# Cutting the fourth tile, placing the final norm by estimates, and storing the output in half-megabyte pieces

## The chip, the cores and the metric

The kernel runs on all eight cores of one Trainium2 chip, one launch, with the same program on each core. The metric is the device time of the slowest core in microseconds (us). Most runs of one kernel agree within 0.3%. A second, slower state appears in some runs whatever the kernel is: the cores of one die show a lower granted TensorE clock and the run is some per cent longer.

Engines are named as in the profile: PE is the TensorE matmul, PEld its weight load, DVE is VectorE, ACT is ScalarE, POOL is GpSimd, SP is SyncE. SPq and ACTq are the queues on which SyncE and ScalarE issue transfers. A *tile* below is one of five groups of token columns, of 256, 512, 512, 512 and 272 columns; a *chunk* is one of eight groups of 128 channels. "The fourth tile" has index 3.

## The reference, cut to what matters

Two decoder layers; each core takes one prompt of 2048 tokens and 16 of the sample tokens. Only the very end is touched by the change: the last feed-forward down projection, its residual add, and the final RMS norm over the 1024 channels.

```python
def rmsnorm(x, g):
    xf = x.astype(jnp.float32)
    y = xf * lax.rsqrt(jnp.mean(xf * xf, axis=-1, keepdims=True) + EPS)
    return (y * g.astype(jnp.float32)).astype(x.dtype)
# ... (mixers, first layer) ...
        x = x + mix
        h = rmsnorm(x, norm_ffn[layer])
        x = x + swiglu(h, ffn_w_gate[layer], ffn_w_up[layer], ffn_w_down[layer])
    return rmsnorm(x, norm_final), ...
```

## The kernel before

Channels lie on partitions and tokens along the free dimension, so the mean over channels needs a sum over partitions. ACT squares each chunk, POOL adds the squares of most chunks into one accumulator, and matmuls with a matrix of ones add what is left and spread the sum to all partitions. ACT then takes Ln and Exp(-0.5 x) to get the reciprocal root ("rstd") in a PSUM bank, and for the chunks that POOL multiplies a second Exp puts it into an SBUF buffer `gtmp` (POOL's chunks get the gain earlier, in a copy on ACT). DVE multiplies the other chunks by gain and rstd at once.

All of this is dripped into the loop of the projection, so that the norm of tile n runs while PE projects tile n+1. In the traces below each engine runs its work in the order in which the program emits it: on core 4, for one, ACT has the Ln and two Exp of `mid`, then the square of chunk 4, its gain copy and the squares of chunks 5, 6 and 7 at 1322.04, 1322.78, 1323.47, 1323.96, 1324.48, 1324.90 and 1325.22 us, and then the gain copy of chunk 7 at 1326.05.

```python
class Norm:
    def square(self, n, c): ...      # ACT Square; POOL adds chunks 0..5; chunks 6, 7 ("direct") go to PE
    def mid(self, n):                # ones-matmuls, Ln, Exp -> gtmp, Exp -> bank; queue 8 multiplies
        ...
    def on_pool(self, n, c):
        return self.final and c in ((1, 4, 7) if n == 4 else (7,))

    POPS = (2, 1, 1, 0, 1, 1, 1, 1)
    POPS4 = (1, 1, 1, 1, 0, 0, 1, 1)

    def step(self, n, m):            # after each chunk m of the projection of tile n
        self.square(n, m)
        if self.on_pool(n, m):       # gain copy on ACT
            sc.op("act", ...Copy, scale=gain...)
        self.pop((self.POPS4 if n == 4 else self.POPS)[m])   # DVE multiplies of the tile before
        if n < 4 and m == 7:
            self.pop_pool(1)

    def before(self, n, m):
        if m == 4 and n > 0:
            self.mid(n - 1)

    def last(self):
        self.mid(4)
        self.pop_pool()
        self.pop(KC)

    def store(self, n, c):
        done = self.stored.setdefault(n, set())
        done.add(c)
        if n < 4:
            if len(done) == KC:      # the whole tile in one store: up to 2 MB
                out_evs.append(sc.dma("sp", o_y[:, xrange_(n)], xT[:, xrange_(n)], ...))
        elif c ^ 1 in done:          # the last tile: four stores of two chunks, 272 KB
            lo = c & ~1
            q_, s_ = ("sp", "out") if lo % 4 == 0 else ("act", "out2")
            ...

def ffn_dn2(l, ga, gb, nm):          # the last down projection
    use_banks(6)
    for n in range(5):
        for m in range(KC):
            nm.before(n, m)
            ...                      # matmuls of chunk m, six per column group
            xacc(bk, bkB, m, n)      # DVE: residual add
            nm.step(n, m)
    nm.end()
    pending[4] = nm.last
```

Of the kernel before, what the change touches and what calls it, by code (L numbers as in the profile page):

```python
# [7 lines left out]
BF16 = mybir.dt.bfloat16  # L8
ALU = mybir.AluOpType
AF = mybir.ActivationFunctionType  # L10
# [5 lines left out]
D = 1024  # L16
KC = 8
SEQ = 2048
NS = 16
T = SEQ + NS  # L20
TT = [(0, 256), (256, 512), (768, 512), (1280, 512), (1792, 272)]
LASTP = (1792, 256)
XOFF = [KC * sum(w_ for _, w_ in TT[:n_]) for n_ in range(len(TT))]
DFF = 2816
# [256 lines left out]
def build_program():  # L281
# [32 lines left out]
    with contextlib.ExitStack() as st:  # L314
        sc = Sched(nc, st, self_sync=SELF_SYNC)

        def sb(name, shape, dt):
            return st.enter_context(nc.sbuf_tensor(name, list(shape), dt))
# [73 lines left out]
        def merge(dsts, srcs):  # L392
            for s_ in srcs:
                evs = ([s_.w] if s_.w is not None else []) + list(s_.r.items())
                for d_ in dsts:
                    for (k_, v_) in evs:
                        if d_.r.get(k_, 0) < v_:
                            d_.r[k_] = v_
# [3 lines left out]
        acc = [sqf[:, i * 512:(i + 1) * 512] for i in range(2)]  # L402
        accb = [sqall[:, i * 1024:i * 1024 + 512] for i in range(2)]
        rng = [sqall[:, 2048 + i * 512:2048 + (i + 1) * 512] for i in range(2)]
        drc = [sqall[:, 3072 + i * 512:3072 + (i + 1) * 512] for i in range(2)]
        accB = [Buf(f"acc{i}") for i in range(2)]
        rngB = [Buf(f"rng{i}") for i in range(2)]
# [5 lines left out]
        def nxt(kind, n):  # L413
            i = st_[kind]
            st_[kind] = (i + 1) % n
            return i
# [153 lines left out]
        def drip(k_):  # L570
            if active:
                active[0].pop(k_)
                if not active[0].q:
                    active.pop()
                    use_banks(8)

        class Norm:

            def __init__(self, gcol, final=False, direct=()):
                self.gcol = gcol  # L580
                self.final = final
                self.direct = direct
                self.q = []
                self.parts = {}
                self.stored = {}
# [53 lines left out]
            def emit(self, n, c):  # L639
                c0, w = TT[n]  # L640
                out = xs(c, n) if self.final else hT[:, c, c0:c0 + w]
                pl = self.on_pool(n, c)
                r_, rB_ = (gtmp[n % 2], gtmpB[n % 2]) if pl else (banks[6 + n % 2], bankB[6 + n % 2])
                if pl:
                    sc.op("pool", lambda E: E.tensor_tensor(
                        out=out, in0=xs(c, n), in1=r_[:, 0:w], op=ALU.mult),
                        reads=[xB[c][n], rB_], writes=[xB[c][n]])
                else:
                    sc.op("dve", lambda E: E.scalar_tensor_tensor(  # L649
                        out=out, in0=xs(c, n), scalar=vecs[:, self.gcol + c:self.gcol + c + 1],  # L650
                        in1=r_[:, 0:w], op0=ALU.mult, op1=ALU.mult),
                        reads=[xB[c][n], rB_, cB["vecs"]],
                        writes=[xB[c][n] if self.final else hB[c][n]])
                if self.final:
                    self.store(n, c)
# [14 lines left out]
            POPS = (2, 1, 1, 0, 1, 1, 1, 1)  # L670
            POPS4 = (1, 1, 1, 1, 0, 0, 1, 1)

            def step(self, n, m):
                self.square(n, m)
                if self.on_pool(n, m):
                    sc.op("act", lambda E: E.activation(
                        out=xs(m, n), in_=xs(m, n), func=AF.Copy,
                        scale=vecs[:, self.gcol + m:self.gcol + m + 1]),
                        reads=[xB[m][n], cB["vecs"]], writes=[xB[m][n]])
                self.pop((self.POPS4 if n == 4 else self.POPS)[m])  # L680
                if n < 4 and m == 7:
                    self.pop_pool(1)

            def before(self, n, m):
                if m == 4 and n > 0:
                    self.mid(n - 1)

# [3 lines left out]
                    self.pop(KC)  # L691

            def last(self):
                self.mid(4)
                if self.final:
                    self.pop_pool()
                    self.pop(KC)
                else:
                    active.append(self)
# [14 lines left out]
        def proj(bk, bkB, wt, wtB, wcol, n, src=None, srcB=None, nk=KC, wstride=None):  # L714
            c0, w = TT[n]
            if src is None:
                need_h(n)
            src_ = hT if src is None else src
            srcB_ = hB if srcB is None else srcB

            def f(E):
                last = None
                for k in range(nk):
                    o = k * wstride + wcol
                    last = E.matmul(bk[:, 0:w], lhsT=wt[:, o:o + 128], rhs=src_[:, k, c0:c0 + w],  # L725
                                    start=(k == 0), stop=(k == nk - 1))
                return last
            wtBs = list(wtB) if isinstance(wtB, (list, tuple)) else [wtB]
            sc.op("pe", f, reads=wtBs + [srcB_[k][n] for k in range(nk)], writes=[bkB])

        def xacc(bk, bkB, m, n):
            c0, w = TT[n]
            sc.op("dve", lambda E: E.tensor_tensor(  # L733
                out=xs(m, n), in0=bk[:, 0:w], in1=xs(m, n), op=ALU.add),
                reads=[bkB, xB[m][n]], writes=[xB[m][n]])

        def out_proj(prefix, nm, slots=None):
            if slots is None:
                slots = [w_acquire(f"{prefix}_{h}") for h in range(2)]
            use_banks(6)  # L740
            for n in range(5):
                for m in range(8):
                    wt, wtB = slots[m // 4]
                    nm.before(n, m)
                    bk, bkB = nbank()
                    proj(bk, bkB, wt, wtB, (m % 4) * 128, n, src=mix, srcB=mB, wstride=512)
                    xacc(bk, bkB, m, n)
                    nm.step(n, m)
            nm.end()
            pending[4] = nm.last  # L750
            w_release()
            w_release()
# [49 lines left out]
        def ffn_dn2(l, ga, gb, nm):  # L802
            wa, waB = w_acquire(f"dn{l}_{ga}")
            wb, wbB = w_acquire(f"dn{l}_{gb}")
            parts = [(wa, 4 * (ga % 2), len(groups[ga])), (wb, 4 * (gb % 2), len(groups[gb]))]
            tot = sum(p_[2] for p_ in parts)
            use_banks(6)
            for n in range(5):
                c0, w = TT[n]
                for m in range(KC):  # L810
                    nm.before(n, m)
                    bk, bkB = nbank()

                    def f(E, bk=bk, m=m, c0=c0, w=w):
                        last = None
                        i = 0
                        for (wt_, s0, nch_) in parts:
                            for jl in range(nch_):
                                last = E.matmul(bk[:, 0:w],  # L819
                                                lhsT=wt_[:, jl * 1024 + m * 128: jl * 1024 + (m + 1) * 128],  # L820
                                                rhs=mix[:, s0 + jl, c0:c0 + w], start=(i == 0), stop=(i == tot - 1))
                                i += 1
                        return last
                    sc.op("pe", f, reads=[waB, wbB] + [mB[s0 + jl][n] for (_, s0, nch_) in parts for jl in range(nch_)],
                          writes=[bkB])
                    xacc(bk, bkB, m, n)
                    nm.step(n, m)
            nm.end()
            pending[4] = nm.last
            w_release()  # L830
            w_release()
# [3 lines left out]
        def ffn(l, nm):  # L835
            G = len(groups)
            ffn_up(l, 0)
            for g in range(1, G):
                ffn_up(l, g)
                if g == G - 1:  # L840
                    act_warm_lnexp()
                    break
                ffn_dn(l, g - 1)
                if l == 0 and g - 1 == 2:
                    w_issue_special("v_1")
            ffn_dn2(l, G - 2, G - 1, nm)

        act_warm_lnexp()
        nbk = {}
# [240 lines left out]
        merge(gtmpB, SB[1:3])  # L1090

        merge(accB + bsB_, sqB)
        out_proj("out0", Norm(VC_NFFN + 0, direct=(7,)), out0)
        merge([wsTB], [SB[3]])
        late_setup()
        ffn(0, Norm(VC_NMIX + 8, direct=(6, 7)))

        wv0, wv0B = w_acquire("v_0")
        wv1, wv1B = w_acquire("v_1")
# [110 lines left out]
                w_release()  # L1210

        act_warm_lnexp()
        out_proj("out1", Norm(VC_NFFN + 8, direct=(7,)))

        out_evs = [ev_pp, ev_ps, ev_cp, ev_cs, ev_v]
        ffn(1, Norm(VC_NFIN, final=True, direct=(6, 7)))
        flush_pending()
        sc.wait("sp", [("out", sc.cnt["out"]), ("out2", sc.cnt["out2"])])
        sc.emit_all()
# [80 lines left out]
```

## Time and profile before

| | before |
|---|---|
| time, median of four runs | 1341.91 us |
| span of the profiled core (4) | 1340.1 us |
| spans of the eight cores | 1338.6 to 1340.1 us |
| granted TensorE clock | 0.991 to 0.993 |
| last projection matmul to end of span | 18.5 us |

The first and the fourth part of the page of the kernel before: busy time of each engine with its share of the span and its instructions, and the chain of waits by engine.

```profile
PE 1289.1 (96%) x7283; PEld 717.6 (54%) x7386; DVE 673.5 (50%) x1190; ACT 346.7 (26%) x669; POOL 168.5 (13%) x213
...
PE 88%; DVE 5%; issue 2%; DMA 1%; ACT 1%; POOL 1%; DVEq 0%; SPq 0%; ACTq 0%; POOLq 0%
```

PE is the limit of the kernel as a whole, but the change leaves all PE work before the last projection as it is. What matters is the stretch in which PE has nothing left to do. The timeline of the kernel before on core 4 shows it; the columns are start in us, busy time, engine, line, operation, out<-in, shape, count, and in brackets the idle time before it with what ended it.

```profile
1278.06 0.20 ACT L556 ACTIVATE small<-small 128x1 f32<-128x1 f32 x1
...
1318.62 2.94 PE L819 MATMUL bank<-mix,wring 128*128 128x272 bf16 x24
...
1322.04 0.65 ACT L623 ACTIVATE bank<-bank,small 128x512 f32<-128x512 f32 x1
...
1322.78 0.60 ACT L627 ACTIVATE gtmp<-bank 128x512 f32<-128x512 f32 x1
1323.47 0.58 ACT L630 ACTIVATE bank<-bank 128x512 f32<-128x512 f32 x1
1323.96 0.42 ACT L605 ACTIVATE sqall<-xTs 128x272 bf16<-128x272 f32 x1
1324.15 0.75 DVE L649 SCALAR_TENSOR_TENSOR xTs<-xTs,vecs_s,bank 128x512 f32<-128x512 f32 x1 [1.55 <-ACT bank L630]
1324.48 0.52 ACT L676 ACTIVATE xTs<-xTs,vecs_s 128x272 f32<-128x272 f32 x1
...
1324.82 0.43 DVE L733 TENSOR_TENSOR xTs<-bank,xTs 128x272 f32<-128x272 f32 x1
1324.90 0.41 ACT L605 ACTIVATE sqall<-xTs 128x272 bf16<-128x272 f32 x1
...
1325.22 0.73 ACT L594 ACTIVATE sqall<-xTs 128x272 bf16<-128x272 f32 x2
...
1326.41 0.53 PE L620 MATMUL bank<-sqall,ones 128*128 128x272 bf16 x3 [4.86 <-POOL sqall L609]
```

The line of 1278.06 is a small warm-up instruction on ACT just before the last projection; it serves below as a common clock. The last projection matmul ends at 1321.56. The last residual add (L733) runs at 1324.82, 3 us later, behind a DVE multiply that waited 1.55 us for the rstd of the fourth tile. On ACT, the Ln and two Exp of the fourth tile (1322.04 to 1324.05) and one gain copy (L676; the copies of chunks 1 and 7, at 1320.22 and 1326.05, are cut) stand among the squares of the last tile.

The store issues begin late: the last DVE multiply of the fourth tile ends at 1329.20, and its 2 MB store is issued at 1329.33. The same timeline, in a call that starts at 1326 us, has the last issues:

```profile
1329.33 2.52 SPq L125 DMA_DIRECT2D yT<-xTs  x3
1330.50 1.62 ACTq L125 DMA_DIRECT2D yT<-xTs  x2
```

The windows of the kernel before on core 4, 2 us each: length, busy time and instruction count of PE, PEld, DVE, ACT and POOL, then the granted clock, the mean busy share of the 16 DMA engines, and GB/s moved. A packet counts whole in the window in which it starts, so that a share can read above 1 and a rate too high.

```profile
1326.00:1328.00 2.00, 0.53 (x3) 0.29 (x3) 2.00 (x4) 1.38 (x3) 1.39 (x2) 0.73 0.41 147
1328.00:1330.00 2.00, 0.00 (x0) 0.00 (x0) 2.00 (x5) 0.38 (x1) 1.87 (x3) 0.50 0.05 12
1330.00:1332.00 2.00, 0.00 (x0) 0.00 (x0) 1.24 (x4) 0.00 (x0) 0.33 (x1) 0.50 0.96 393
1332.00:1334.00 2.00, 0.00 (x0) 0.00 (x0) 0.00 (x0) 0.00 (x0) 0.00 (x0) 0.50 1.12 467
1334.00:1336.00 2.00, 0.00 (x0) 0.00 (x0) 0.00 (x0) 0.00 (x0) 0.00 (x0) 0.50 0.87 299
1336.00:1338.00 2.00, 0.00 (x0) 0.00 (x0) 0.00 (x0) 0.00 (x0) 0.00 (x0) 0.50 1.08 334
1338.00:1340.10 2.10, 0.00 (x0) 0.00 (x0) 0.00 (x0) 0.00 (x0) 0.00 (x0) 0.50 0.32 107
```

From 1328 to 1330 the DMA engines are all but idle (a share of 0.05) while DVE works without a pause (2.00 of 2.00 us); from 1332 on no engine computes and until 1338 DMA is full (0.87 to 1.12). So transfers wait for arithmetic, and then the end waits for transfers. The DMA issues of the kernel before: operation, count, size, and median us from issue to landing.

```profile
yT<-xTs SPq DMA_DIRECT2D x3, 2048.0 KB, 6.7
...
yT<-xTs SPq DMA_DIRECT2D x1, 1024.0 KB, 3.9
yT<-xTs SPq DMA_DIRECT2D x2, 272.0 KB, 8.8
yT<-xTs ACTq DMA_DIRECT2D x2, 272.0 KB, 8.0
```

The 272 KB stores take longer (8.8 and 8.0 us) than the 2 MB ones (6.7): they are issued from 1329.81 to 1331.37, right behind the last 2 MB store (1329.33), which lands at 1336.58.

### The profile page before, as it was taken

What the parts mean: (1) busy time and instruction counts of PE and PEld (TensorE: products, weight loads), DVE (VectorE), ACT (ScalarE), POOL (GpSimd) and SP (SyncE); (2) the same over time, 40 slices, a digit from 0 to 9 for tenths busy, and PEclk for the clock granted to TensorE, in tenths of its full rate; (3) what the DMA queues carried; (4) which work ended last, traced back from release to release, by engine and by line L of the source; (5) the groups of instructions that cost most, each with busy time, mean ns of one, the idle gap of its engine ahead of it and who ended that gap; (6) DMA issues with size and microseconds to landing.
All of it is one profiled execution on the core that took longest, in us unless ns stands there. A gap on an engine that the chain in (4) does not pass through costs nothing.

```text
span 1340.1 us, 21630 instructions; the slowest of 8 cores (1338.6 to 1340.1 us)
## 1 busy us (share of the span) xinstructions
PE 1289.1 (96%) x7283; PEld 717.6 (54%) x7386; DVE 673.5 (50%) x1190; ACT 346.7 (26%) x669; POOL 168.5 (13%) x213
## 2 busy tenths in 40 slices
PE   4998999999999999999999999999999999999994
PEld 2554545555555555556454665555655556555552
DVE  2887567223527235532764775721262532645166
ACT  3522443111010110012576334411101011010154
POOL 3200153000000000000521005300000000000054
PEclk9999999999999999999999999999999999999998
DMA  9524204122111233102160101231132111320105
GB/s 260 117 48 64 48 2 64 32 43 53 33 32 33 42 54 63 33 16 43 22 127 1 34 6 28 44 52 33 32 54 42 33 32 32 55 42 16 33 33 222
DMA packets 11179, 68.67 MB, mean 51 GB/s; under 512 B 2064, under 2 KB 2192, under 8 KB 4912
## 3 DMA queue, kind: packets, MB, share of 16 engines
q0 software_dynamic: 6912, 47.19, 21.3%
q1 hardware_dynamic: 3584, 19.47, 4.2%
q8 instruction: 63, 1.03, 0.3%
q10 hardware_dynamic: 576, 0.62, 0.2%
q14 instruction: 44, 0.36, 0.1%
HBM read 105.84 MB, written 9.18 MB: 86 GB/s over the span
## 4 chain that ended last, share of the span: by engine, by line
PE 88%; DVE 5%; issue 2%; DMA 1%; ACT 1%; POOL 1%; DVEq 0%; SPq 0%; ACTq 0%; POOLq 0%
PE bank L725 60%; PE bank L795 17%; PE bank L819 4%; PE bank L1130 4%; PE bank L956 2%; DMA xTs<-xT 1%; DVE xTs L649 1%; PE bank L1186 1%; DVE R L1071 1%; DVE R L1068 1%; PE bank L620 0%; DVE xTs L733 0%; DVE R L1051 0%; DVE gtmp L913 0%; PE bank L877 0%
## 5 line engine op out<-in xcount | busy, mean ns | idle before, releaser
L725 PE MATMUL bank<-hTs,wring 128*128 128x512 bf16 (+2 forms) x4105 | 731.1, 338 | 6.9 <-DVE R L1043 3.0
L725 PEld LDWEIGHTS bank<-hTs,wring 128*128 128x128 bf16 x4160 | 406.3, 98 | 323.1 <-issue 9.2
L776 DVE TENSOR_TENSOR mix<-bank,gtmp 128x512 bf16<-128x512 f32 (+2 forms) x220 | 129.4, 588 | 465.3 <-PE bank L725 459.8
L733 DVE TENSOR_TENSOR xTs<-bank,xTs 128x512 f32<-128x512 f32 (+2 forms) x480 | 279.0, 587 | 90.8 <-PE bank L725 34.7
L773 ACT ACTIVATE gtmp<-bank 128x512 f32<-128x512 f32 (+2 forms) x220 | 113.0, 515 | 712.3 <-PE bank L725 694.2
L795 PE MATMUL bank<-mix,wring 128*128 128x512 bf16 (+2 forms) x1264 | 223.8, 337 | 0.8
L795 PEld LDWEIGHTS bank<-mix,wring 128*128 128x128 bf16 x1280 | 125.4, 98 | 98.0
L125 POOL DMA_DIRECT2D wring<-wts x46 | 25.1, 547 | 956.3 <-PE bank L725 443.6
L609 POOL TENSOR_TENSOR sqall<-sqall 128x512 f32<-128x512 f32 (+5 forms) x110 | 106.6, 969 | 129.6 <-ACT sqall L605 123.2
L725 PE MATMUL bank<-mix,wring 128*128 128x512 bf16 (+2 forms) x632 | 112.6, 337 | 0.4
L725 PEld LDWEIGHTS bank<-mix,wring 128*128 128x128 bf16 x640 | 62.6, 98 | 49.0
L819 PE MATMUL bank<-mix,wring 128*128 128x512 bf16 (+2 forms) x472 | 85.0, 337 | 0.4
L605 ACT ACTIVATE sqall<-xTs 128x512 bf16<-128x512 f32 (+2 forms) x110 | 59.7, 546 | 70.6 <-DVE xTs L733 60.8
L649 DVE SCALAR_TENSOR_TENSOR hTs<-xTs,vecs_s,bank 128x512 bf16<-128x512 f32 (+2 forms) x120 | 73.8, 638 | 2.0 <-ACT bank L630 1.7
L819 PEld LDWEIGHTS bank<-mix,wring 128*128 128x128 bf16 x480 | 47.0, 98 | 36.6
L956 PE MATMUL bank<-hTs,wring 128*128 128x512 bf16 (+2 forms) x157 | 30.7, 351 | 3.9 <-ACT R L975 1.9
L1130 PE MATMUL bank<-mix,hTs 128*128 128x512 bf16 (+1 forms) x135 | 31.9, 379 | 0.1
L1130 PE MATMUL bank<-wring,hTs 128*128 128x512 bf16 (+1 forms) x131 | 31.5, 379 | 0.3
L1174 ACT ACTIVATE gtmp<-bank 128x512 f32<-128x512 f32 (+2 forms) x40 | 20.6, 514 | 42.6 <-PE bank L725 26.7
L725 PE MATMUL bank<-hTs,mix 128*128 128x512 bf16 (+2 forms) x156 | 30.5, 337 | 0.2
L1153 DVE SCALAR_TENSOR_TENSOR R<-mix,rsv 128x1024 bf16<-128x1024 f32 (+1 forms) x17 | 21.8, 1284 | 15.1 <-POOL rsv L1150 15.1
L1206 DVE TENSOR_TENSOR mix<-bank,gtmp 128x512 bf16<-128x512 f32 (+2 forms) x40 | 23.5, 589 | 7.4 <-DVE bank L1197 5.0
(96 smaller groups left out, 481.9 us busy)
## 6 DMA issues: line engine op xcount, KB each, us to landing
wring<-wts POOLq DMA_DIRECT2D x38, 1024.0 KB, 9.8
xTs<-xT SPq DMA_DIRECT2D x3, 2048.0 KB, 25.1
yT<-xTs SPq DMA_DIRECT2D x3, 2048.0 KB, 6.7
wring<-wts POOLq DMA_DIRECT2D x4, 768.0 KB, 10.0
wring<-wts POOLq DMA_DIRECT2D x4, 512.0 KB, 8.2
mix<-wts POOLq DMA_DIRECT2D x2, 1024.0 KB, 19.6
xTs<-xT SPq DMA_DIRECT2D x1, 1088.0 KB, 33.2
xTs<-xT SPq DMA_DIRECT2D x4, 256.0 KB, 7.0
```

The source lines that it names most:

```text
L125: E.dma_start(out=out, in_=in_, **kw).then_inc(s, 16)
L605: sc.op("act", lambda E: E.activation(out=rng[i][:, 0:w], in_=xs(c, n), func=AF.Square), reads=[xB[c][n]], writes=[rngB[i]])
L609: sc.op("pool", lambda E: E.tensor_tensor(out=dst[:, 0:w], in0=acc[a][:, 0:w], in1=rng[i][:, 0:w], op=ALU.add), reads=[accB[a], rngB[i]], ...
L649: sc.op("dve", lambda E: E.scalar_tensor_tensor(out=out, in0=xs(c, n), scalar=vecs[:, self.gcol + c:self.gcol + c + 1], in1=r_[:, 0:w], op ...
L725: last = E.matmul(bk[:, 0:w], lhsT=wt[:, o:o + 128], rhs=src_[:, k, c0:c0 + w], start=(k == 0), stop=(k == nk - 1))
L733: sc.op("dve", lambda E: E.tensor_tensor(out=xs(m, n), in0=bk[:, 0:w], in1=xs(m, n), op=ALU.add), reads=[bkB, xB[m][n]], writes=[xB[m][n]])
L773: sc.op("act", lambda E, bg_=bg_, gi=gi, w=w: E.activation(out=gtmp[gi][:, 0:w], in_=bg_[:, 0:w], func=AF.Silu), reads=[bgB], writes=[gtmp ...
L776: sc.op("dve", lambda E, bu_=bu_, gi=gi, w=w, c0=c0, slot=slot: E.tensor_tensor(out=mix[:, slot, c0:c0 + w], in0=bu_[:, 0:w], in1=gtmp[gi] ...
L795: last = E.matmul(bk[:, 0:w], lhsT=wt[:, jl * 1024 + m * 128: jl * 1024 + (m + 1) * 128], rhs=mix[:, slot, c0:c0 + w], start=(jl == 0), st ...
L819: last = E.matmul(bk[:, 0:w], lhsT=wt_[:, jl * 1024 + m * 128: jl * 1024 + (m + 1) * 128], rhs=mix[:, s0 + jl, c0:c0 + w], start=(i == 0), ...
L956: last = E.matmul(bks[g][0][:, 0:w], lhsT=wt[:, k * 512 + g * 128:k * 512 + (g + 1) * 128], rhs=hT[:, k, c0:c0 + w], start=(k == 0), stop= ...
L1130: last = E.matmul(bk[0:ntok, :], lhsT=hT[:, k, t0:t0 + ntok], rhs=wv[:, k * 512:(k + 1) * 512], start=(k == 0), stop=(k == KC - 1))
```

## The change

Its intent is to shorten this tail: start the norm of the end of the sequence earlier, spread its arithmetic better, and give bytes to the DMA engines as soon as they are final. It has four parts, all in the last projection with the final norm. The other norms keep the old code and order (as `NormOld`).

1. The fourth tile is cut into two segments of 256 columns; six segments in all.
2. In the last three segments all eight squares go straight to ones-matmuls, so POOL no longer adds squares there. POOL takes two or three multiplies of each late segment instead, and from the fourth segment on it also scales its chunks by the gain, which ACT did before.
3. The emission order is set by running estimates of each engine's time, in place of the fixed `POPS` tables.
4. Stores are about 0.5 MB: two chunks of a 512-column segment, four of a narrower one.

The core of the diff, cut (bookkeeping of the estimates, buffer slots, `NormOld`, and the matching un-layout on the host are left out):

```diff
+        def last_tiles():
+            l_ = []
+            for n, cut in ((0, (256,)), (1, (512,)), (2, (512,)), (3, (256, 256)), (4, (272,))):
+                ...
+        LAG = 2.0
+
         class Norm:
...
+            def dr(self, s):
+                return tuple(range(KC)) if self.final and s.w < 512 and s.i else self.direct
+
+            def pool_set(self, s):
+                return ((7,), (7,), (3, 5, 7), (1, 3, 5), (1, 3, 5), (0, 2), (0, 2))[s.i] if self.final else ()
...
+            def fit(self):
+                for _ in range(3):
+                    e = [(s, c) for (s, c) in self.q if c not in self.pool_set(s)]
+                    if not e:
+                        return
+                    s = e[0][0]
+                    t_ = max(self.tdve, self.rstd[s.i])
+                    if t_ > self.tdve + 0.05 or t_ + s.w / 960 + 0.11 > self.tpe + self.dur + LAG:
+                        return
+                    self.pop(1)
+
+            def before(self, s, m):
+                p_ = s.i - 1
+                if p_ >= 0 and p_ not in self.mid_done and (m >= 6 or self.ready[p_] <= self.tpe):
+                    self.mid(self.segs[p_])
+
+            def step(self, s, m):
+                ...
+                self.square(s, m)
+                if m in self.pool_set(s):
+                    if s.i < 3:
+                        ...                                  # gain copy on ACT, as before
+                    else:
+                        sc.op("pool", lambda E: E.tensor_scalar(
+                            out=s.x(m), in0=s.x(m), scalar1=vecs[...], scalar2=None, op0=ALU.mult), ...)
+                self.fit()
+                if m == 7 or len(self.dr(s)) == KC:
+                    self.pop_pool()
...
+            def store(self, s, c):
+                done = self.stored.setdefault(s.i, [])
+                done.append(c)
+                k_ = 2 if s.w == 512 else 4
+                lo = c - c % k_
+                if all(c_ in done for c_ in range(lo, lo + k_)):
+                    q_, s_ = ("act", "out2") if (s.n == 4 and lo) else ("sp", "out")
+                    ...
+                    out_evs.append(sc.dma(q_, dst, src, reads=s.b[lo:lo + k_], sem=s_))
```

## The prediction

> What bounds the kernel. The page of the kernel before shows PE busy 96% of 1340.1 us, and its chain of waits is 88% PE. The change touches only the last FFN down projection with the final norm and the output stores (all earlier work keeps its order), so only the end can move. The timeline there: last projection matmul (L819) ends at 1321.6; the span ends at 1340.1. These 18.5 us run: the last residual adds (L733) queue on DVE behind a norm multiply (L649) that waits for the rstd of the fourth tile (idle 1.55 us), so the last add starts only at 1324.8; its square ends 1325.95; ones-matmuls 1326.4 to 1326.9 (PE had idled 4.9 us); Ln, Exp, Exp to 1328.5; DVE multiplies, 7 of 512 columns (0.65 us apart) then 5 of 272 (0.42 us apart), to 1331.2. The 2 MB store of the fourth tile is released only at 1328.6, and the last tile's four 272 KB stores follow; the windows show DMA at 300 to 470 GB/s from 1330 to about 1338.5. 3.2 MB at 360 GB/s is 8.9 us: the end is a store drain, not arithmetic.
>
> What the change does. The fourth tile is cut into two of 256 columns, the last three segments feed all eight squares to ones-matmuls (no POOL accumulation), norm work is placed by a running estimate of each engine, POOL takes two or three multiplies per late segment, stores become about 0.5 MB.
>
> Costs on PE: cutting is nearly free (0.109 us per 256-column matmul against 0.219 for 512). Before the last projection ends, 3+8+8 ones-matmuls replace 3+3: about 1.1 us. The last projection matmul should end near 1322.5[...].
>
> Gains (estimates from the durations above): the last add ends near 1323.1, square near 1324.1 (ACT is busy with the rstd of the segment before), ones 1324.4, Ln/Exp/Exp 1325.9, six DVE multiplies of 272 columns end about 1328.4, 2.8 us earlier than before. The larger gain is the drain: by then all but 0.5 MB is written or in flight. The issue table has a 1 MB store landing in 3.9 us and a 2 MB one in 6.7, so 1.1 us fixed plus 2.8 per MB; a 0.54 MB store needs about 2.6. With issue and end, the span should end near 1332.2 instead of 1340.1. [...]
>
> Predicted time: 1334.0 us, 80% range 1332.0 to 1336.8, 0.6% faster. Chance of over 2% faster 0.5%, within 2% 98.5%, over 2% slower 1%.
>
> What would show it: last projection matmul at 1322 to 1323; last add within 1 us of it; last DVE multiply at 1328 to 1329; end 3.5 to 4 us later, against 8.9 before; no PE idle over 0.5 us inside the projection; stores of the fourth tile's halves begun before 1325.5.
>
> What would make it wrong: DVE falling behind in the 256-column segments (a matmul group lasts 0.66 us, an add plus a multiply of 512 columns 1.25), stalling PE on banks; ones-matmuls waiting in PE's order for late squares; POOL's multiplies (1.27 us for 512 columns) and gain scalings, never timed here, running late and holding stores; the 1 KB pieces of the halves' stores or more issues per queue slowing the drain. Each would cost 0.5 to 3 us.

The sum: the span from 1340.1 to 1332.2 us, 7.9 us less, and so a time of 1334.0 us. The 360 GB/s is an estimate and agrees with the trace: 3.2 MB over the 8.9 us from the last multiply (1331.2) to the end (1340.1), within the 300 to 470 GB/s of the windows. The matmuls of 256 columns start 0.109 us apart on core 4 of before, those of 512 columns 0.216 us (median). The size of each risk, and that smaller pieces or more issues might slow the drain, were estimates; what pieces of 1 KB did is measured below.

## The result, and the profile after

| | before | after |
|---|---|---|
| median of all runs | 1341.78 us (15 runs) | 1334.25 us (10 runs) |
| fast runs, after over before | | 0.9943 (95%: 0.9933 to 0.9952) |
| profiled core, span | 1340.1 us (core 4) | 1332.3 us (core 7) |
| spans of the cores | 1338.6 to 1340.1 us | 1330.7 to 1332.3 us |

Every ratio here and below is the mean time of one kernel's fast runs over that of the other's fast runs of the same rounds, so it is not quite the ratio of the medians. The change is worth 0.6%, well inside 2%. The same two parts of the page of the kernel after:

```profile
PE 1298.5 (97%) x7452; PEld 724.0 (54%) x7452; DVE 672.6 (50%) x1200; ACT 346.6 (26%) x678; POOL 170.7 (13%) x217
...
PE 91%; DVE 4%; issue 2%; DMA 1%; ACT 1%; POOL 0%; DVEq 0%; SPq 0%; ACTq 0%; POOLq 0%
```

PE has more to do and the span is still shorter. (Part of the 9.4 us of added PE time is not real work: the trace of before lacks some matmul records, as its 7283 matmuls beside 7386 weight loads show.) The end of the timeline of the kernel after on core 7, with the warm-up instruction first:

```profile
1277.30 0.20 ACT L559 ACTIVATE small<-small 128x1 f32<-128x1 f32 x1
...
1283.18 0.52 PE L680 MATMUL bank<-sqall,ones 128*128 128x256 bf16 x3 [0.34 <-POOL sqall L664]
...
1319.28 2.94 PE L1041 MATMUL bank<-mix,wring 128*128 128x272 bf16 x24
...
1319.53 8.06 SPq L126 DMA_DIRECT2D yT<-xTs  x5
...
1320.96 0.43 ACT L683 ACTIVATE bank<-bank,small 128x256 f32<-128x256 f32 x1
...
1322.29 1.38 ACT L650 ACTIVATE sqall<-xTs 128x272 bf16<-128x272 f32 x4
1322.33 0.44 DVE L956 TENSOR_TENSOR xTs<-bank,xTs 128x272 f32<-128x272 f32 x1 [0.25 <-PE bank L1041]
...
1322.86 1.23 PE L680 MATMUL bank<-sqall,ones 128*128 128x272 bf16 x4 [0.17 <-ACT sqall L650]
1322.86 2.05 DVE L710 SCALAR_TENSOR_TENSOR xTs<-xTs,vecs_s,bank 128x256 f32<-128x256 f32 x5
...
1325.77 2.54 DVE L710 SCALAR_TENSOR_TENSOR xTs<-xTs,vecs_s,bank 128x272 f32<-128x272 f32 x6 [0.86 <-ACT bank L691]
1328.39 0.35 ACTq L126 DMA_DIRECT2D yT<-xTs  x1
```

The last add now starts 0.11 us after the last projection matmul, the last four squares run right behind it, and the ones-matmuls wait 0.17 us instead of 4.86. The DVE multiplies of the segment before (L710, 1322.86) stand behind the last add, not in front of it, and the last six run from 1325.77 to 1328.31. Stores go out from 1319.53 on; the last is issued at 1328.39. The windows of the kernel after on core 7, with the same columns as before:

```profile
1320.00:1322.00 2.00, 2.00 (x20) 1.69 (x18) 1.68 (x5) 1.50 (x4) 2.00 (x3) 1.00 0.81 275
1322.00:1324.00 2.00, 1.70 (x10) 0.72 (x8) 1.66 (x5) 1.66 (x5) 1.95 (x4) 1.00 0.78 270
1324.00:1326.00 2.00, 0.09 (x1) 0.00 (x0) 1.14 (x4) 1.24 (x3) 0.55 (x2) 1.00 0.65 207
1326.00:1328.00 2.00, 0.00 (x0) 0.00 (x0) 2.00 (x6) 0.00 (x0) 1.10 (x2) 0.54 0.97 312
1328.00:1330.00 2.00, 0.00 (x0) 0.00 (x0) 0.31 (x1) 0.00 (x0) 0.00 (x0) 0.50 1.00 402
1330.00:1332.30 2.30, 0.00 (x0) 0.00 (x0) 0.00 (x0) 0.00 (x0) 0.00 (x0) 0.50 0.38 151
```

The hole in the DMA share (0.05 in 1328 to 1330 before) is gone, and only the last window and most of the one before it are pure transfer. The issues of the kernel after:

```profile
yT<-xTs SPq DMA_DIRECT2D x14, 512.0 KB, 3.4
...
yT<-xTs SPq DMA_DIRECT2D x1, 544.0 KB, 3.6
yT<-xTs ACTq DMA_DIRECT2D x1, 544.0 KB, 3.6
```

**A common clock.** Cores reach the last projection at slightly different times (the warm-up instruction starts between 1276.4 and 1278.1 us on the cores of before, 1275.6 and 1277.4 after). Counted from that instruction, most steps of one kernel's arithmetic repeat to about 0.02 us between cores (the last rstd of before only to 0.3 us), so these steps can be compared far below the noise of the total. The end repeats less well: it lies between 61.99 and 62.27 on the cores of before and between 54.62 and 55.52 on those of after, so a difference of a few tenths between two ends may be scatter. Mean over eight cores, in us after the warm-up instruction:

| step | before | after | difference |
|---|---|---|---|
| last projection matmul ends | 43.50 | 44.93 | +1.43 |
| last residual add ends | 47.19 | 45.48 | -1.71 |
| last square ends | 47.89 | 46.37 | -1.52 |
| last rstd (Exp) ends | 50.60 | 48.37 | -2.23 |
| last DVE multiply ends | 53.18 | 51.01 | -2.17 |
| span ends | 62.13 | 54.99 | -7.14 |
| last multiply to end | 8.95 | 3.98 | -4.97 |
| still to be moved at the last multiply | 2.70 MB | 1.03 MB | -1.67 MB |

So 7.1 of the 7.5 us are in the tail: 2.2 us from arithmetic that ends earlier and 5.0 us from a shorter wait for transfers after it. The remaining 0.4 us is the mean difference of the warm-up instruction's own start (1277.05 against 1276.65), which is smaller than its spread of 1.7 us between cores; that it belongs to the change is not established.

### The profile page after: what moved, and what is told of

Read it like the earlier page. It is cut to its first block, busy times and chain, and to the rows that moved or that the text cites. A ratio compares the mean times of both kernels' runs of the same rounds, so it can differ in the third digit from the quotient of the medians.

```text
span 1332.3 us, 21955 instructions; the slowest of 8 cores (1330.7 to 1332.3 us)
## 1 busy us (share of the span) xinstructions
PE 1298.5 (97%) x7452; PEld 724.0 (54%) x7452; DVE 672.6 (50%) x1200; ACT 346.6 (26%) x678; POOL 170.7 (13%) x217
## 3 DMA queue, kind: packets, MB, share of 16 engines
q0 software_dynamic: 6912, 47.19, 21.5%
q8 instruction: 63, 1.03, 0.3%
## 4 chain that ended last, share of the span: by engine, by line
PE 91%; DVE 4%; issue 2%; DMA 1%; ACT 1%; POOL 0%; DVEq 0%; SPq 0%; ACTq 0%; POOLq 0%
PE bank L943 60%; PE bank L1017 17%; PE bank L1041 6%; PE bank L1351 4%; PE bank L1177 2%; DMA xTs<-xT 1%; PE bank L1098 1%; PE bank L1407 1%; DVE R L1292 1%; DVE R L1289 1%; PE bank L835 0%; DVE R L1272 0%; DVE gtmp L1134 0%; DVE wsT_s L1134 0%; PE bank L680 0%
## 5 line engine op out<-in xcount | busy, mean ns | idle before, releaser
L998 DVE TENSOR_TENSOR mix<-bank,gtmp 128x512 bf16<-128x512 f32 (+2 forms) x220 | 129.4, 588 | 465.4 <-PE bank L943 458.5
L1017 PEld LDWEIGHTS bank<-mix,wring 128*128 128x128 bf16 x1280 | 125.3, 98 | 98.1
L824 POOL TENSOR_TENSOR sqall<-sqall 128x512 f32<-128x512 f32 (+5 forms) x85 | 82.3, 968 | 81.1 <-ACT sqall L820 76.8
L943 PEld LDWEIGHTS bank<-mix,wring 128*128 128x128 bf16 x640 | 62.5, 98 | 49.0
L1041 PEld LDWEIGHTS bank<-mix,wring 128*128 128x128 bf16 x528 | 51.6, 98 | 32.2
L820 ACT ACTIVATE sqall<-xTs 128x512 bf16<-128x512 f32 (+2 forms) x85 | 46.0, 546 | 58.6 <-DVE xTs L956 51.5
```

The source lines that it names most:

```text
L820: sc.op("act", lambda E: E.activation(out=rng[i][:, 0:w], in_=xs(c, n), func=AF.Square), reads=[xB[c][n]], writes=[rngB[i]])
L824: sc.op("pool", lambda E: E.tensor_tensor(out=dst[:, 0:w], in0=acc[a][:, 0:w], in1=rng[i][:, 0:w], op=ALU.add), reads=[accB[a], rngB[i]], ...
L943: last = E.matmul(bk[:, 0:w], lhsT=wt[:, o:o + 128], rhs=src_[:, k, c0:c0 + w], start=(k == 0), stop=(k == nk - 1))
L998: sc.op("dve", lambda E, bu_=bu_, gi=gi, w=w, c0=c0, slot=slot: E.tensor_tensor(out=mix[:, slot, c0:c0 + w], in0=bu_[:, 0:w], in1=gtmp[gi] ...
L1017: last = E.matmul(bk[:, 0:w], lhsT=wt[:, jl * 1024 + m * 128: jl * 1024 + (m + 1) * 128], rhs=mix[:, slot, c0:c0 + w], start=(jl == 0), st ...
L1041: last = E.matmul(bk[:, 0:w], lhsT=wt_[:, jl * 1024 + m * 128: jl * 1024 + (m + 1) * 128], rhs=mix[:, s0 + jl, c0:c0 + w], start=(i == 0), ...
```

## The experiments

The main theory (drain): the end waits for bytes, so it follows the time at which bytes are released and their number, not the arithmetic. Its rivals: the end follows the last multiply, and the arithmetic is delayed by the last residual add that stands behind a waiting multiply on DVE (the first row of the prediction); or one of the four parts alone does all of it. Experiments are numbered e1 to e12; all gave correct results. The clean cores named are those of the die that showed no dip of the granted clock in the last 60 us while PE worked; all values on the common clock.

### e1: the old kernel with the new store sizes

```diff
                 if n < 4:
-                    if len(done) == KC:
-                        out_evs.append(sc.dma("sp", o_y[:, xrange_(n)], xT[:, xrange_(n)], ...))
+                    k_ = 2 if n else 4
+                    lo = c - c % k_
+                    if all(c_ in done for c_ in range(lo, lo + k_)):
+                        out_evs.append(sc.dma("sp", o_y[:, xrange_(n, lo, lo + k_)], ...))
```

> The kernel before with one edit: each whole tile leaves in stores of about 0.5 MB (pairs of chunks, or four chunks of the first tile) as soon as these chunks are normalised; the arithmetic and its order are untouched. Theory D (the end is a store drain, because the 2 MB of the fourth tile are held back until their eighth chunk is done): arithmetic ends where it did (last multiply 54.3 us after the projection starts), but the fourth tile's first half MB leaves about 3 us earlier, and the end comes 2.5 to 4.5 us earlier (ratio to before 0.9966 to 0.998). Rival A (the arithmetic chain sets the end and the stores only follow it): within 0.7 us of before.

Measured: 1339.6 us against 1342.35 of before in the same rounds, ratio 0.9982 (0.9969 to 0.9995). The arithmetic did not move (last multiply 53.17 against 53.18); the end came at 59.81 against 62.13, 2.3 us earlier, because 1.55 MB instead of 2.70 MB were left. The store size is a part of the gain by itself, at or just under the low end of what the drain theory expected.

### e2: the new kernel with the old store sizes

```diff
-                k_ = 2 if s.w == 512 else 4
+                k_ = 2 if s.n == 4 else KC          # whole tiles; the last tile in pairs
                 ...
+                    if s.n == 3:                    # both halves wait until both are done
+                        group = [g_ for g_ in self.segs if g_.n == 3]
+                        if any(len(self.stored.get(g_.i, ())) < KC for g_ in group):
+                            return
```

> The kernel after with one edit: stores in the pieces of before (one per tile, the fourth tile's two halves both held until the second half is done, the last tile in four pairs on two queues); arithmetic untouched. Theory D: the fourth tile's 2 MB leave only when its second half is multiplied, about 1.5 us before the first chunks of the last tile, so 3.2 MB drain behind it; the end comes 2.5 to 4 us later than after, so the time is about 1337.5 (ratio to before 0.996 to 0.998). Rival A: within 0.7 us of after (ratio about 0.9943).

Measured: 1336.99 us, ratio 0.9963 (0.995 to 0.9976); die 0 had a dip of the clock (0.95 on the mean from 1305 to 1322 us) which put its last projection matmul 0.9 us later, but not its end. On the clean cores 4 to 7 the last multiply stays at 51.04 and the end is at 57.49: 2.5 us after that of the new kernel, the least that the drain theory allowed, and 4.6 us before that of the old one. The two parts nearly add up: 2.3 (e1) and 4.6 (e2) make 6.9 of 7.14 us. About a third of the gain is the store size, two thirds the earlier and reordered arithmetic.

### e3: the old kernel with the last adds freed

The one multiply of the fourth tile that stands before the last add on DVE goes behind it.

```diff
-                self.pop((self.POPS4 if n == 4 else self.POPS)[m])
+                pops = (1, 1, 1, 1, 0, 0, 0, 0) if self.final else self.POPS4
+                self.pop((pops if n == 4 else self.POPS)[m])
```

> The kernel before with the norm multiplies of the fourth tile all placed behind the last residual add on DVE (before: one of them, which waits for its rstd, stands in front of it). The prediction's reading, theory V (the last add stuck on DVE delays the last tile's rstd): the last add ends about 2.5 us earlier and the last square and the ones-matmuls 1 to 2 us earlier. Rival S (ScalarE's order holds the squares: it runs Ln, Exp, Exp of 512 columns and two gain copies among them without a gap): the add comes earlier but the last square moves by less than 0.4 us. The span changes by less than 0.7 us under both, since the fourth tile's store is not released earlier.

Measured: 1342.08 us, ratio 1.0004 (0.9991 to 1.0017). The last add ended at 44.89 instead of 47.19, 2.3 us earlier, and the last square ended at 47.89, exactly as before. The end was at 62.00. Four lines of the timeline of e3 on core 4 show why:

```profile
1320.64 1.83 DVE L734 TENSOR_TENSOR xTs<-bank,xTs 128x272 f32<-128x272 f32 x5
...
1321.56 0.64 ACT L623 ACTIVATE bank<-bank,small 128x512 f32<-128x512 f32 x1
...
1322.99 0.58 ACT L630 ACTIVATE bank<-bank 128x512 f32<-128x512 f32 x1
...
1324.74 0.73 ACT L594 ACTIVATE sqall<-xTs 128x272 bf16<-128x272 f32 x2
```

All adds are done by 1322.47, and the last two squares still run only at 1324.74. ACT works its list in order here: Ln, Exp and Exp of the fourth tile, 512 columns wide and 2.01 us long (1321.56 to 1323.57), then squares and gain copies of the last tile one after the other. The wait of DVE that looked like the cause was real but had a slower neighbour beside it. The rival theory of the last add falls, and with it one reason in the prediction.

DVE is not cleared altogether. Before the Ln, ACT waited twice for earlier adds of the last tile (0.30 and 0.58 us before its squares in the kernel before). Those adds stand behind multiplies of the third tile, which wait for nothing; e3 leaves them there, so what they cost was not tested.

### e4: the new kernel without the cut

```diff
-            ... (3, (256, 256)), (4, (272,))):
+            ... (3, (512,)), (4, (272,))):
-                return ((7,), (7,), (3, 5, 7), (1, 3, 5), (1, 3, 5), (0, 2), (0, 2))[s.i] if self.final else ()
+                return ((7,), (7,), (3, 5, 7), (3, 5, 7), (0, 2))[s.i] if self.final else ()
-                    if s.i < 3:
+                    if s.i < 4:                     # gain copies of the fourth tile on ACT
```

(The buffer for the last tile's squares had to grow, and the fourth tile goes back to POOL accumulation.)

> The kernel after with the fourth tile left whole (512 columns, squares added on POOL and gain copies on ScalarE as the third tile has them; its store in four pairs; the last tile keeps its eight direct squares). Theory C (the cut itself earns part of the gain, because half of the fourth tile is normalised while the projection still runs): five multiplies of 512 columns start only after the last adds, the last multiply ends about 1.5 us later than after, and the span ends 1 to 2.5 us later. Rival F (finer stores and the reordering earn all of it): within 0.7 us of after, or a little earlier, as about 1.1 us of ones-matmuls fall away on PE.

Measured: 1338.17 us, ratio 0.9971 (0.9957 to 0.9986). On clean cores the last multiply ended at 50.51, which is 0.5 us *earlier* than with the cut. Against the expectation: without the cut PE has fewer ones-matmuls to run, and the last projection matmul ends 1.2 us earlier (43.75 against 44.93). Yet the end is at 57.17, 2.2 us later than with the cut, since 1.80 MB instead of 1.03 MB are still to be moved. The cut, with the direct squares of the fourth tile that come with it, pays only by making half of that tile final earlier; for the arithmetic the two together are a small loss, and the run does not separate them. A theory in which the end follows the last multiply gives the wrong sign here.

### e5: the old kernel with more arithmetic

e3, and all eight multiplies of the last tile on DVE.

```diff
-                return self.final and c in ((1, 4, 7) if n == 4 else (7,))
+                return self.final and c in (() if n == 4 else (7,))
```

> The kernel before with the multiplies of the fourth tile behind the last add (as in the run of that name) and with all eight multiplies of the last tile on DVE, none on POOL, so that its three gain copies fall away on ScalarE. Theory S (ScalarE's order sets the last square): the last square comes about 0.5 us earlier, since one copy between the squares is gone; rival: unchanged. Theory D (store drain sets the end): the three more multiplies of 0.42 us on DVE make the last multiply about 1.0 us later, but the end moves by less than 0.4 us, as 3 MB are still queued then; rival A (the arithmetic chain sets the end): the end is about 1 us later.

Measured: 1341.9 us, ratio 0.9998 (0.9985 to 1.0011). On the clean cores 0 to 3 the last multiply ended at 54.18, 1.0 us later than in the old kernel, and the end was at 62.07 against 62.13. A whole microsecond of added DVE work at the end cost nothing, while the DMA engines had a backlog (2.2 MB at the last multiply): this is the direct test of "a store drain, not arithmetic". It shows ACT's part as well: without gain copies for the last tile the last square ended 0.56 us earlier (47.33 against 47.89 of e3), about one 0.52 us copy.

### e6: gain scaling of the last segment back on ACT

```diff
-                    if s.i < 3:
+                    if s.i < 3 or s.i == 5:         # ACT copies also for the last segment
```

> The kernel after with one edit: the two gain scalings of the last tile run on ScalarE again (0.52 us each) instead of on POOL; same order else. Theory S (ScalarE's queue carries the last tile's chain): the second copy pushes the Ln, Exp, Exp of the segment before and with them the last four squares, so the last square, the last multiply and the end come 0.4 to 0.8 us later. Rival V (the chain hangs on the adds of DVE): the last square moves by less than 0.15 us.

Measured: 1335.72 us, ratio 0.9952 (0.9939 to 0.9965). For e6, e7 and e8 die 1 of the chip had a dip of the clock that put its last projection matmul at 45.9 to 46.5 and the times about 1 us up, so their tails are read on die 0. There the last square moved to 47.07, the last multiply from 51.01 to 51.70, and the end only from 54.99 to 55.11. So two copies on ACT cost 0.6 to 0.7 us of arithmetic and at most 0.1 us of time, which is within the scatter of the ends: after the change, too, the last multiply is partly hidden by transfers in flight.

### e7: last stores of half the size

```diff
-                k_ = 2 if s.w == 512 else 4
+                k_ = 2 if s.w == 512 or s.n == 4 else 4
-                    q_, s_ = ("act", "out2") if (s.n == 4 and lo) else ("sp", "out")
+                    q_, s_ = ("act", "out2") if (s.n == 4 and lo % 4) else ("sp", "out")
```

> The kernel after with one edit: the last tile leaves in four stores of 272 KB, alternating over two queues, instead of two of 544 KB. Theory D': with the earlier data gone, the time from the last multiply to the end (3.98 us mean over the cores) is the fixed cost of a store plus its bytes, so half the bytes make it 0.4 to 0.8 us shorter. Rival: it is a fixed landing time or a backlog, and it changes by less than 0.2 us.

Measured: 1335.97 us, ratio 0.9955 (0.9943 to 0.9966); end at 54.96 against 54.99 on clean cores. Halving the last stores gains nothing, where 0.4 to 0.8 us had been expected.

### e8: one Exp fewer at the very end

For the last segment DVE reads the rstd from `gtmp` in SBUF, and the Exp into the PSUM bank is dropped.

```diff
-                sc.op("act", ...Exp, out=bk...)
+                if not (self.final and s.i == 5):
+                    sc.op("act", ...Exp, out=bk...)
...
-                        in1=banks[6 + s.i % 2][:, 0:w], ...
+                        in1=(gtmp[gi] if s.i == 5 else banks[6 + s.i % 2])[:, 0:w], ...
```

> The kernel after with one edit: for the last tile only one Exp, into SBUF, which DVE and POOL both read (after: a second Exp into the bank for DVE). Theory N (after the change the last tile's arithmetic chain sets the end): DVE starts 0.45 us earlier and the end comes 0.3 to 0.5 us earlier. Rivals: DVE and POOL slow each other when both read SBUF (multiplies longer than 0.42 us apart on DVE or 0.74 us on POOL), which eats the gain; or a backlog of stores sets the end and it does not move.

Measured: 1335.24 us, ratio 0.9952 (0.9941 to 0.9964). The rstd came 0.48 us earlier (47.89), and the last multiply 0.55 us *later* (51.56). The next two lines are one line's instructions, first in e8 on core 0, then in the kernel after on core 7: count, shortest, median and longest duration in ns, and first and last start.

```profile
L713 DVE SCALAR_TENSOR_TENSOR xTs<-xTs,vecs_s,gtmp x6: 490/497/997, 1325.8 to 1328.9; 128x272 f32<-128x272 f32 x6
```

```profile
L710 DVE SCALAR_TENSOR_TENSOR xTs<-xTs,vecs_s,bank x6: 491/491/497, 1325.8 to 1327.8; 128x272 f32<-128x272 f32 x6
```

With the second input in PSUM every multiply took 0.49 us. With both in SBUF, two of the six took 1.0 us while POOL multiplied beside them, the six together 3.57 us instead of 2.54, and POOL's own two took 0.79 and 0.95 us instead of 0.76. So the Exp that looks superfluous kept DVE's multiplies short here. Why they are longer without it is not shown: in e8 DVE and POOL both read SBUF, and they read the same buffer, and the run does not separate the two. The end moved by 0.06 us (55.05).

### e9: the reciprocal root before the last squares

The squares and gain scalings of two chunks of the last segment are held back until the rstd work of the segment before is emitted.

```diff
+                if self.final and s.i == 5 and m in (2, 3):
+                    self.held.append((s, m))        # emitted right after mid() of segment 4
+                else:
+                    self.square_gain(s, m)
...
```

> The kernel after with one edit: on ScalarE the squares of the last tile's third and fourth chunk stand behind the Ln, Exp, Exp of the segment before instead of in front of them. Theory D'' (after the change the end is still the store drain, now of what is released in the last 8 us): that segment's rstd comes 0.7 to 1.0 us earlier, DVE multiplies it between the last adds, its 1 MB leaves 0.5 to 0.9 us earlier, the last multiply stays within 0.4 us, and the end comes 0.3 to 0.7 us earlier on a core without a clock dip. Rival: the end hangs on the last release alone and moves as the last multiply does.

Measured: 1335.31 us, ratio 0.9952 (0.994 to 0.9965). On all eight cores the last add moved from 45.48 to 46.85, the last square from 46.37 to 47.38, the last multiply from 51.01 to 52.01 and the end from 54.99 to 55.79. The edit made worse what it was to cure: the estimates now placed five multiplies of the segment before ahead of the last two adds on DVE. They did not wait for their rstd, but took 2.1 us there (1.26 and 0.86 us on core 0). Here, other than in e3, the squares moved with the adds. The full microsecond of arithmetic cost 0.8 us.

### e10: a shorter permitted lag of DVE

```diff
-        LAG = 2.0
+        LAG = 0.5
```

> The kernel after with the one constant of its placement rule changed: multiplies may run 0.5 us past the estimated end of the next projection group instead of 2.0. They then stand one behind each add from the third segment on, and two of the rstd chains are placed earlier on all engines. Theory D'': stores are released more evenly and earlier, so the end comes 0.3 to 1.0 us earlier, if PE does not wait for squares at the earlier ones-matmuls (its last projection matmul may come up to 0.5 us later). Rival L (the 2 us lag is what makes the order work): adds queue behind multiplies that wait for their rstd, PE stalls on banks, and the end comes over 1 us later.

Measured: 1334.21 us, ratio 0.9943 (0.993 to 0.9957). Last multiply 50.90 (0.1 us earlier), end 54.56 (0.43 us earlier than after, where the cores of e10 alone spread from 54.20 to 55.11); rival L falls. In total time it cannot be told from the kernel after.

### e11: squares added on POOL again

```diff
             def dr(self, s):
-                return tuple(range(KC)) if self.final and s.w < 512 and s.i else self.direct
+                return self.direct
```

> The kernel after with one edit: the last three segments add six of their eight squares on POOL again (as before the change) instead of giving all eight to the ones-matmuls; POOL keeps the gain scalings and its multiplies. Theory P (the direct squares are what frees POOL for its new work): POOL then has about 27 us of work from 1308 us on (five adds of 0.67, three scalings of 0.92 and three multiplies of 0.71 us for each 256 columns), against 19 us of time, so its last multiply and the end come 5 to 9 us later, about where before ended. Rival: POOL has the slack; the end within 1 us of after.

Measured: 1344.65 us, ratio 1.0021 (1.0008 to 1.0034), slower than the old kernel. POOL's timeline in e11 on core 5 is an unbroken row of adds, gain scalings and multiplies:

```profile
1315.49 3.74 POOL L705 TENSOR_TENSOR xTs<-xTs,gtmp 128x512 f32<-128x512 f32 x3
...
1323.13 0.67 POOL L664 TENSOR_TENSOR sqall<-sqall 128x256 f32<-128x256 f32 x1
...
1324.65 0.93 POOL L761 TENSOR_SCALAR xTs<-xTs,vecs_s 128x256 f32<-128x256 f32 x1
...
1332.86 0.70 POOL L664 TENSOR_TENSOR sqall<-sqall 128x272 bf16<-128x272 f32 x1 [0.20 <-POOL sqall L664]
```

The ones-matmuls wait for its sums in PE's own order (3.68 us before those at 1324.82 on core 5), so the last projection matmul ends at 51.31 instead of 44.93, and the span at 65.47, 10.5 us later (5 to 9 had been expected). Sending the squares straight to PE costs about 1 us of matmuls and is what makes POOL's new work affordable: POOL could not add the squares here and do the multiplies and gains of the late segments in time.

### e12: the points that helped, together

```diff
-        LAG = 2.0
+        LAG = 0.5
-                return (..., (1, 3, 5), (0, 2), (0, 2))[s.i] if self.final else ()
+                return (..., (1, 3, 5), (0, 2, 4), (0, 2))[s.i] if self.final else ()
```

(and the stores of e7)

> The kernel after with three edits: the 0.5 us placement lag, the last tile's stores in pairs over two queues, and POOL takes three of the last tile's multiplies instead of two. If both the last multiply and the bytes still queued set the end (what the runs so far suggest, each alone moving it by 0 to 0.4 us), the two shrink together: the last multiply comes 0.4 to 0.6 us earlier than after and the end 0.6 to 1.2 us earlier on cores without a clock dip; time 1333.2 to 1333.8, ratio to before 0.9937. If one fixed thing (the landing of the last store, or the engines' drain rate) remains, the end comes 0.4 us earlier or less.

Measured: 1334.07 us, ratio 0.9938 (0.9924 to 0.9952). On the clean cores 4 to 7 the last multiply is at 50.45 and the end at 54.39, 0.6 us before the mean of the kernel after (0.45 us before that of its own cores 4 to 7). The total time is not distinguishable from it, as the intervals overlap.

### The runs side by side

Us on the common clock, clean cores; the gap is from the last multiply to the end, and the last column is what the DMA engines still moved in it.

| kernel | last add | last square | last multiply | end | gap | MB left |
|---|---|---|---|---|---|---|
| before | 47.19 | 47.89 | 53.18 | 62.13 | 8.95 | 2.70 |
| e3 last adds freed | 44.89 | 47.89 | 52.89 | 62.00 | 9.11 | 2.70 |
| e5 more arithmetic | 44.88 | 47.33 | 54.18 | 62.07 | 7.89 | 2.2 |
| e1 fine stores | 47.18 | 47.89 | 53.17 | 59.81 | 6.64 | 1.55 |
| e2 coarse stores | 45.52 | 46.41 | 51.04 | 57.49 | 6.45 | 1.46 |
| e4 no cut | 44.30 | 45.55 | 50.51 | 57.17 | 6.66 | 1.80 |
| after | 45.48 | 46.37 | 51.01 | 54.99 | 3.98 | 1.03 |
| e9 rstd earlier | 46.85 | 47.38 | 52.01 | 55.79 | 3.78 | 0.91 |
| e12 combined | 45.70 | 46.22 | 50.45 | 54.39 | 3.94 | 0.86 |
| e11 POOL adds | 51.85 | 55.24 | 61.14 | 65.47 | 4.33 | 1.18 |

A straight line through the gaps of all kernels but e1 and e2 is 0.9 us plus 3.0 us per MB left; each of these lies within 0.5 us of it. By that line the 1.67 MB that are no longer left would be worth 5.1 us; the gap shrank by 5.0. e1 and e2 lie 1.1 and 1.2 us above the line. Both have large stores or slow arithmetic before a last tile stored in four pieces, but e7 and e12 store the last tile in pieces of that size without such a penalty. The traces show where the excess lies: with each packet shared out over its own time, the bytes left (but for the last 0.04 MB) moved at 335 GB/s in e1 and 321 in e2 (mean of the clean cores), against 414 in the kernel after and 400 in e12. Why they moved slower stays open.

## Why the prediction was right, and where it was not

The total was 1334.0 predicted and 1334.25 measured, inside the range, and the class (within 2%) was right. That it is so close is in part luck: the forecast takes 7.9 us from the span, the tail gave 7.14, and the other 0.4 us of the measured 7.5 come from cores that reached the last projection earlier, which the prediction did not foresee. Point by point:

- **"The end is a store drain, not arithmetic": right.** e5 added 1.0 us of arithmetic to the old kernel without moving its end, e1 moved the end by 2.3 us without touching the arithmetic, and in e4 the end moved against the last multiply.
- **PE's cost: right in kind, 0.5 us short.** The last projection matmul was to end near 1322.5, which is 0.9 us later than before. On the common clock it came 1.43 us later: about 1.1 us of ones-matmuls, as predicted, and 0.34 us in which PE waits for POOL's sum at the first tile's ones-matmuls, since the estimates place these too early (line of 1283.18). No PE wait within the projection exceeded 0.5 us, as predicted.
- **The last multiply 2.8 us earlier: 2.17 us.** The predicted sum was +0.9 us on PE and -3.7 us from the last projection matmul to the last multiply. Measured: +1.43 and -3.60. So the term that was mis-sized is PE's, above all.
- **The reason given for the late squares: wrong.** The prediction read the chain as "the last residual adds queue on DVE behind a norm multiply that waits for the rstd of the fourth tile". e3 took that away: the add came 2.3 us earlier and the last square not at all. ACT's in-order list was the limit: Ln and two Exp over 512 columns plus gain copies among the squares. The change relieves ACT: the Ln now starts 1.26 us before the last projection matmul ends (1320.96 against 1322.22), where it had started 0.48 us after it, and the late gain copies are on POOL. That the pieces are half as wide matters little, since in e4, with 512 columns, the last square still ends only 1.80 us after the last projection matmul (after: 1.44; before: 4.39). What is left over, an estimated 2 us of the 2.95, goes to the new order on DVE and ACT; no run isolates it. That is why the predicted gain came although the reason was wrong. e5 and e6 show the share of the gain copies: one fewer is worth 0.56 us, two back cost 0.6 to 0.7 us.
- **"By then all but 0.5 MB is written or in flight": true as worded, but the wrong sum was drawn from it; another term made this good by luck.** Only the last 544 KB store was still to be issued (at 1328.39), but with what was in flight 1.03 MB were still to be moved at the last multiply. The wait after it was 3.98 us where the forecast had 3.8, because the forecast let one 0.54 MB store take 2.6 us and added 1.2 us for issue and end, while on core 7 the last store took 3.6 us to land behind the others and issue and end took 0.4 us. The fit over the kernels gives 0.9 us plus 3.0 us per MB of everything left. The prediction's own pair from the issue table, 1.1 us plus 2.8 us per MB, was close to that fit; it was applied to one store instead of to the backlog.
- **Stores of the halves before 1325.5, last add within 1 us of the last projection matmul, end 3.5 to 4 us after the last multiply: all seen** (stores from 1319.53, add within 0.55 us, 3.98 us).
- **The named risks.** DVE did not fall behind. POOL did hold the first half's two stores: they went out at 1319.53 and 1320.22, 0.1 us after its multiplies of chunks 3 and 5, and these had started only at 1318.03, behind gain scalings (the half's DVE multiplies ended at 1319.83); what that cost the end is not shown. Halves are stored in 1 KB pieces and moved at 330 to 350 GB/s at full DMA share, against about 390 to 410 GB/s for pieces of 4 KB; on some 2 MB of halves this is an estimated 0.9 us of transfer time (2.1 MB at 340 against 400 GB/s), partly hidden under arithmetic. That risk existed and was smaller than the gain.

What the parts are worth: e1 gives 2.3 us to the store size alone and e2 4.6 us to the rest. Within the rest, the cut with its direct squares is worth 2.2 us (e4) through earlier bytes only, and POOL's new work needs the direct squares (e11: without them the end comes 3.3 us after that of the old kernel). The placement by estimates was not undone alone; e9 and e10 only shift it. What bounds the tail after the change is mixed: 1.0 us of arithmetic more cost 0.8 us (e9), 0.55 to 0.69 us more cost 0.1 us (e6, e8), and no variation that was tried made the tail more than 0.6 us shorter.

## What to carry to other kernels

At the end of a kernel count the bytes that are not yet moved when the last arithmetic ends: here each MB left cost about 3.0 us across the kernels tried, and making bytes final earlier (by cutting the tile before the last, and by storing in pieces) brought 5.0 of the 7.1 us. A wait that the profile names is a cause only if nothing else on the way is as late: look at what the next engine's in-order list was doing in that time, and undo the wait alone before building on it. Work moved to a free engine must be paid for there; the POOL multiplies were affordable here only because the square sums left POOL for matmuls that cost PE about 1 us (with the sums back on POOL the end came 10.5 us later, e11).

## What else was measured of the hardware here

- With each packet shared out over its own time, the stores of 2 MB of the kernel before moved at up to 430 GB/s for 1 us (428 to 430 on the eight cores) and 424 GB/s for 3 us on every core. (The windows read higher, up to 508 GB/s in that of 1324 to 1326 us, because a packet counts whole where it starts.)
- Pieces of 1 KB moved at 330 to 350 GB/s, pieces of 4 KB at 390 to 410 GB/s, both at full DMA share (core 7 of the kernel after).
- For these stores from the SP and ACT queues the fit over the drains was 0.9 us plus 3.0 us per MB, and a 512 KB store landed in as little as 2.6 us (core 7 of the kernel after).
- On POOL the one-input gain scaling took 0.912 to 0.967 us for 128x256 and 128x272, and the two-input add of the same sizes 0.67 to 0.70 us: the one with fewer inputs was the slower one.
- Eight cores with PE busy 96% of the time were granted a mean clock of 0.988 to 0.997 in the fast runs of before and after; in the two slow runs of the kernel after the cores of one die fell to 0.855 to 0.877.
- A DVE multiply of 0.49 us took up to 1.0 us while POOL multiplied beside it and both read SBUF (e8).
